# Attention states scaled in batches on VectorE, a later context transposition and six sums off GpSimd in a one-layer mixer and FFN kernel

## The chip, the cores and the metric

The kernel runs on one core of one Trainium2 chip. The metric is device time in microseconds, the median of three runs. "The profile" is the record of one further execution of the same program. TensorE is PE in it, its weight loads PEld, VectorE is DVE, ScalarE is ACT, GpSimd is POOL and SyncE is SP.

## The reference, cut to what matters

One layer: a mixer of three head groups (gated linear attention in both directions, a 2-D Fourier mix, a bidirectional linear recurrence) that share one input and one output projection, then a SwiGLU FFN. The 256 context tokens are used only for the states with which the scans of the 1024 latent tokens begin.

```python
def gla_scan(q, k, v, log_a, s0):            # forward; backward on flipped inputs
    ...
    b = jnp.cumsum(gc, axis=3)
    q_t = qc * jnp.exp(b)
    k_t = kc * jnp.exp(-b)
    k_end = kc * jnp.exp(b_last - b)
    attn = jnp.where(mask, jnp.einsum('nbhik,nbhjk->nbhij', q_t, k_t), 0.0)
    o_intra = jnp.einsum('nbhij,nbhjv->nbhiv', attn, vc)

    def step(s, inp):
        q_n, k_n, v_n, d_n = inp
        o_n = jnp.einsum('bhik,bhkv->bhiv', q_n, s)
        s_new = s * d_n[:, :, 0, :, None] + jnp.einsum('bhjk,bhjv->bhkv', k_n, v_n)
        return s_new, o_n
    ...
def gla_final_state(k, v, log_a):            # the context's state
    b = jnp.cumsum(log_a, axis=1)
    w = jnp.exp(b[:, -1:] - b)
    return jnp.einsum('bthk,bthv->bhkv', k * w, v)

def combine_groups(o_gla, z_og, g_gla, z_f, h_rg, z_rg):
    y_gla = gla_norm_gate(o_gla, z_og, g_gla)
    y_f = fourier_mix(z_f)
    y_rg = h_rg * jax.nn.gelu(z_rg.astype(jnp.float32))
    return jnp.concatenate([y_gla, y_f, y_rg], axis=-1).astype(z_og.dtype)

# latent_mixer: s_f, s_b, hf0, hb0 come from the context
    o_f, _ = gla_scan(q, k, v, la_f, s_f)
    o_b_rev, _ = gla_scan(rev(q), rev(k), rev(v), rev(la_b), s_b)
    h_f, h_b_rev = rglru_bidir(u, w_rg_a, b_rg_a, w_rg_x, b_rg_x, rg_lam, hf0, hb0)
    return combine_groups(o_f + rev(o_b_rev), z_og, g_gla, z_f, h_f + rev(h_b_rev), z_rg)
```

## The kernel before

All products are fp32 split into a high and a low part, so each is three matmuls (`mm3`, lines L84, L85 and L86). The input projection is made in tiles: `z` tiles (weights stationary or moving, 512 columns) and `zn` tiles (256 columns, tokens on the partitions). `z_v1` makes the second half of v in `zn` tiles, `vN` and `vNc` hold v of the latent tokens and of the context.

**The context's states.** For each of two head pairs p and two directions d, `ctx_exp` makes the weighted keys `b_c` (scan L438, exponential, product L443, on DVE and ACT), `ctx_tr` transposes them on PE (L449) and copies them to `kw_c` on DVE (L451), and `ctx_state` multiplies them with v (L459) and copies the state `s_ctx` (L462).

**The latent states.** `gla_states(p)` runs per head pair. `gla_kT` transposes the weighted keys `Kt` (L509). `gla_kv` takes a direction and a half q of the sequence, which has four steps in q=0 and three in q=1: products `kv` on PE (L527), then a chain `tt` on DVE (L532), each step from the one before. Each `tt` is also scaled by `gs` into the state tile `St` that the attention reads (L518, two instructions of 64x128 on ACT for two heads). The state of the context, scaled, is the first entry: with it 8 entries in each of 4 (p, d), 64 instructions on ACT.

**The attention blocks.** `gla_block(p, n)` makes one of 8 blocks of 128 tokens: the decayed queries `qx` (L571; direction 0 on DVE from `qT`, direction 1 on POOL from `qTs`, a copy of `qT` with its halves of partitions exchanged by DMA), `attn` (L575, PE), mask `am` (L577, L578, DVE), then `o` (L582 reads `St` and `qx`, L583 reads `am` and v). Direction 1 runs from the end, so block 0 needs the last entry of its chain. Between the blocks `fill` puts `z` tiles on PE: the queries of the second head pair, then the Fourier input.

**The recurrence.** `rg_ctx` and `rg_gates` make gates (`gate_ps`, L600, PE) with ACT functions behind, `rg_scan` scans on DVE (L644) and adds the two directions on POOL (L648, 128x1024, twice). `ada_row` sums eight slices of a weight (L658, DVE, `ada_acc`) and brings them to PE as `row_ps` (L669).

**The Fourier part.** `fourier` folds its input on DVE and POOL (`ze`, `zo`, `zfold`, L816 to L824), multiplies on PE (`Z_ps` L837, `y_ps` L850). `z_rg` makes `yfr` by a gelu on ACT from the next `zn` tiles, multiplied with the recurrence on DVE (L807). The output projection `o_ps` and the FFN (`prod`, `dn`) follow.

The program is written in the order of the functions; a scheduler with a model of the engines then sets each engine's order, within what pools allow: PSUM has 4 tiles of the kind `mm` and 4 of the kind `aux`. An engine works its own queue strictly in that order. So an instruction that waits holds up all that stands behind it on its engine. Line numbers are those of the kernel before; in the kernel after they are one to two higher from L518 on.

Of the kernel before, what the change touches and what calls it, by code (L numbers as in the profile page):

```python
# [16 lines left out]
P = 128  # L17
# [21 lines left out]
def tile_trunk(ctx: ExitStack, tc: tile.TileContext, A: dict):  # L39
    nc = tc.nc  # L40
    V, S, G, PE = nc.vector, nc.scalar, nc.gpsimd, nc.tensor
# [12 lines left out]
    def hp(shape=(P, 512), dt=F32, name="hp"):  # L54
        t = pool.tile(list(shape), dt, tag="hp", bufs=NHP, name=name)
        names["hp"].add(t.name)
        return t

    def sm(name, n=1):
        bufs = {3: 4, 4: 8, 8: 14}.get(n, 24)  # L60
        return pool.tile([P, n], F32, tag=f"sm{n}", bufs=bufs, name=name)

    def mm(name="mm"):
        return psum.tile([P, 512], F32, tag="mm", bufs=4, name=name)

    def aux(name="aux"):
        return psum.tile([P, 512], F32, tag="aux", bufs=4, name=name)
# [27 lines left out]
    def fl(ap, d):  # L95
        return ap[:, ::-1] if d else ap
# [129 lines left out]
    R = [slice(h * 64, (h + 1) * 64) for h in range(2)]  # L226
# [132 lines left out]
    def z_v1(blocks, c=False):  # L359
        z_N(w_v[1], 256, lambda ps, m: S.copy(vNc[1] if c else vN[1][m // 4][:, m % 4:m % 4 + 2, :], ps), blocks, c)  # L360
# [68 lines left out]
    s_ctx = [[None] * 2 for _ in range(2)]  # L429
# [35 lines left out]
    Ex, Kt, St = [[None] * 2 for _ in range(2)], [[None] * 2 for _ in range(2)], [[None] * 2 for _ in range(2)]  # L465

    def kt_begin(p):
        Kt[p] = [pg(name="Kt") for _ in range(2)]
        exchange(Kt[p][1], kT[p])
# [31 lines left out]
    def order(q):  # L501
        return range(4 * q, min(4 * q + 4, 7))
# [9 lines left out]
        return kn, last  # L512

    def gla_kv(p, d, q, kn, gs, tprev):
        def state(m, t):
            n = (7 - m) if d else m
            for h in range(2):
                S.mul(St[p][h ^ d][R[h], n, :], t[R[h]], gs[R[h], m:m + 1])  # L518

        if q == 0:  # L520
            state(0, s_ctx[p][d])
            tprev = s_ctx[p][d]
        kv = aux("kv")
        for i, m in enumerate(order(q)):
            n = (7 - m) if d else m
            for h in range(2):
                PE.matmul(kv[R[h], i * P:(i + 1) * P], kn[:, i * P + h * 64:i * P + (h + 1) * 64],  # L527
                          vN[p][n // 4][:, n % 4, (h ^ d) * P:((h ^ d) + 1) * P], start=True, stop=True)
        t4 = hp((P, 4, P), name="tt")
        for i, m in enumerate(order(q)):  # L530
            tt = t4[:, i, :]
            V.scalar_tensor_tensor(tt, tprev, gs[:, m:m + 1], kv[:, i * P:(i + 1) * P], op0=ALU.mult, op1=ALU.add)  # L532
            state(m + 1, tt)
            tprev = tt
        return tprev

    def gla_states(p):
# [14 lines left out]
    qT, qTs = [], []  # L552
# [13 lines left out]
    def gla_block(p, n):  # L566
        cs = slice(n * P, (n + 1) * P)
        qx, am = hp((P, 2, P), name="qx"), hp((P, 2, P), name="am")
        for d in range(2):
            for h in range(2):  # L570
                (G if d else V).tensor_mul(qx[R[h], h ^ d, :], (qTs if d else qT)[p][R[h], cs], Ex[p][d][R[h], cs])  # L571
        at = [aux("attn")[:, 0:256].rearrange("p (d i) -> p d i", d=2) for _ in range(2)]
        for d in range(2):
            for h in range(2):
                mark = PE.matmul(at[h][:, d, :], Kt[p][d][R[h], cs], qx[R[h], h ^ d, :], start=True, stop=True)  # L575
        for h in range(2):
            V.tensor_mul(am[:, h, :], at[h][:, 0, :], wmask)  # L577
            V.copy_predicated(am[:, h, :], imask, at[1 - h][:, 1, :])  # L578
        o = mm("o")
        for h in range(2):  # L580
            oc = o[:, h * P:(h + 1) * P]
            PE.matmul(oc, qx[:, h, :], St[p][h][:, n, :], start=True, stop=False)  # L582
            PE.matmul(oc, am[:, h, :], vN[p][n // 4][:, n % 4, h * P:(h + 1) * P], start=False, stop=True)  # L583
        ss = sm("oss", 2)
        jk = pool.tile([P, P], mybir.dt.bfloat16, tag="jk", bufs=1, name="jk")
        for h in range(2):
            S.activation(jk, o[:, h * P:(h + 1) * P], AF.Square, accum_out=ss[:, h:h + 1])
        r = rstd(ss, P, "ors", 2)
        if n % 4 == 0:
            on[p][n // 4] = pg((P, 4, 256), name="on")  # L590
        for h in range(2):
            V.tensor_scalar_mul(on[p][n // 4][:, n % 4, h * P:(h + 1) * P], o[:, h * P:(h + 1) * P], r[:, h:h + 1])
        return mark
# [21 lines left out]
    hR = []  # L615
# [25 lines left out]
    def rg_scan(blk, d, part):  # L641
        a, tr, ti = part
        rg_input(a, tr, ti)
        V.tensor_tensor_scan(fl(a, d), fl(a, d), fl(ti, d), h0[:, 2 * d + blk:][:, 0:1], op0=ALU.mult, op1=ALU.add)  # L644
        if d == 0:
            hR.append(a)
        else:
            G.tensor_add(hR[blk], hR[blk], a)  # L648


    def ada_row(c0, fn):
# [65 lines left out]
        vN[1][i] = pg((P, 4, 256), name="vN")  # L717
    w_q = [w_T(C_Q)]
    bs = [ctx_exp(p, d) for p, d in PD]
    z_v1(range(4))  # L720
    kws = [ctx_tr(b) for b in bs]
    for (p, d), kw in zip(PD, kws):
        ctx_state(p, d, kw)
    z_v1(range(4, 8))
    kt_begin(0)
    w_q.append(w_T(C_Q + P))
    def z_steps(w, h, ev):
# [47 lines left out]
    zf = [pg(name="zf") for _ in range(2)]  # L775
# [33 lines left out]
    def fourier(zf, blk):  # L809


        e, o = pg(name="ze")[:, 0:513], hp(name="zo")
        V.tensor_copy(e[:, 0:513:512], zf[:, 0:513:512])
        G.memset(o[:, 0:1], 0.0)
        rv = zf[:, 513:1024][:, ::-1]
        V.tensor_add(e[:, 1:512], zf[:, 1:512], rv)  # L816
        G.tensor_sub(o[:, 1:512], zf[:, 1:512], rv)
        f = pg((P, 4, 256), name="zfold")
        er, orv = e[:, 257:513][:, ::-1], o[:, 257:512][:, ::-1]
        V.tensor_add(f[:, 0, :], e[:, 0:256], er)  # L820
        V.tensor_sub(f[:, 1, :], e[:, 0:256], er)
        G.memset(f[:, 2:4, 0:1], 0.0)
        G.tensor_sub(f[:, 2, 1:], o[:, 1:256], orv)
        G.tensor_add(f[:, 3, 1:], o[:, 1:256], orv)  # L824
        cols = sm("fcol", 3)
        jk = hp(name="fjk")[:, 0:256]
        V.tensor_mul(jk, f[:, 0, :], alt)
        V.tensor_reduce(cols[:, 0:1], jk, axis=mybir.AxisListType.X, op=ALU.add)
        V.tensor_add(cols[:, 0:1], cols[:, 0:1], e[:, 256:257])
        V.tensor_copy(cols[:, 1:2], e[:, 256:257])  # L830
        V.tensor_copy(cols[:, 2:3], o[:, 256:257])
        Z = pg((P, 4, 2, P), name="Zcs")
        for s in range(2):
            ps = aux("Z_ps")
            for q in range(2):
                for i in range(2):
                    PE.matmul(ps[:, (2 * q + i) * P:(2 * q + i + 1) * P], f[:, 2 * s + q, i * P:(i + 1) * P], (Cd, Sd)[s],  # L837
                              start=True, stop=True)
            S.copy(Z[:, 2 * s:2 * s + 2].rearrange("p q i n -> p (q i n)"), ps)
        pc = aux("fc_ps")  # L840
        PE.matmul(pc[:, 0:2], Cd, cols[:, 0:2], start=True, stop=True)
        PE.matmul(pc[:, 2:3], Sd, cols[:, 2:3], start=True, stop=True)
        cc = sm("fcc", 3)
        V.tensor_copy(cc, pc[:, 0:3])
        yy = []
        for s in range(2):
            ps = aux("y_ps")
            for q in range(2):
                for i in range(2):
                    PE.matmul(ps[:, q * 256:(q + 1) * 256], Z[:, 2 * s + q, i, :], dft[s][:, q, i, :], start=i == 0, stop=i == 1)  # L850
            yy.append(ps.rearrange("p (q m) -> p q m", q=2))
        c, s = yy
        t = hp((P, 2, 256), name="yc")
        V.scalar_tensor_tensor(t[:, 0, :], alt, cc[:, 1:2], c[:, 0, :], op0=ALU.mult, op1=ALU.add)
        V.scalar_tensor_tensor(t[:, 1, :], alt, cc[:, 2:3], s[:, 1, :], op0=ALU.mult, op1=ALU.add)
        parts = (t[:, 0, :], s[:, 0, :]), (c[:, 1, :], t[:, 1, :])
        for q, (yc, ys) in enumerate(parts):
            for j in range(2):
                m = slice(j * P, (j + 1) * P)
                V.tensor_sub(yfr[j][:, blk, q::2], yc[:, m], ys[:, m])  # L860
            m = slice(1 - q, 129 - q)
            V.tensor_add(yfr[3][:, blk, q::2][:, ::-1], yc[:, m], ys[:, m])
            m = slice(129 - q, 256)
            V.tensor_add(yfr[2][:, blk, 2 - q::2][:, ::-1], yc[:, m], ys[:, m])
        V.tensor_copy(yfr[2][:, blk, 0:1], cc[:, 0:1])
# [450 lines left out]
    w = t_split(0)  # L1316
# [6 lines left out]
    for f in range(NFF):  # L1323
# [13 lines left out]
        w = wn  # L1337
# [92 lines left out]
```

## Time and profile before

| | |
|---|---|
| median of 3 runs | 1158.56 us (1156.19 to 1158.96) |
| the profiled execution, its own time | 1158.2 us |
| its span, first to last instruction | 1156.1 us |
| PE busy | 1090.0 us, 94% |
| DVE busy | 808.6 us, 70% |
| ACT busy | 504.6 us, 44% |
| POOL busy | 107.1 us, 9% |
| mean granted clock of TensorE | 0.968 |

The profiled execution is 2.1 us longer than its span; the stretch of the program that the change touches lies between 150 and 350 us of it, and the output projection begins at 381 us. Shares of busy time are means over stages with different limits. What is read is therefore where PE stands idle inside that stretch, what ended the idle time, and at which clock PE went on: 1.00 is the upper of two levels (2.4 GHz), 0.50 the lower (1.2 GHz), and a mean between them tells how much of a window was spent at each.

### The profile page before, as it was taken

The numbers are of one execution on the slowest core, as the hardware profiler recorded it, in microseconds if no ns is written. First come the engines' busy times: TensorE is split into PE (matmuls) and PEld (weight loads), VectorE is DVE, ScalarE is ACT, GpSimd is POOL, SyncE is SP. The second block draws the span as 40 slices with busy tenths as digits, with TensorE's granted clock in tenths as the row PEclk, the third lists the DMA queues.
The fourth block names the chain that finished last, engine by engine and source line by source line (L and its number), as shares of the span: only waits on it lengthen the run. The fifth ranks groups of instructions, "written<-read, shape, count | busy, mean of one in ns | idle before, by whom it ended". The sixth has DMA issues, their size and how long they took to land.

```text
span 1156.1 us, 15092 instructions
## 1 busy us (share of the span) xinstructions
PE 1090.0 (94%) x5514; PEld 904.8 (78%) x5514; DVE 808.6 (70%) x1383; ACT 504.6 (44%) x962; POOL 107.1 (9%) x133
## 2 busy tenths in 40 slices
PE   4899999989999999959999999999999999999877
PEld 2798886867789888748878888888888888888755
DVE  3474693648878366897788778776777658782795
ACT  3451867486364356653323233333323244470251
POOL 2210001214220001550000000000000000000100
PEclk8899998989999999969999999999999999999989
DMA  9803211213526223342382324232423479581681
GB/s 329 293 20 113 71 47 45 50 26 106 167 76 240 71 94 109 110 127 60 97 283 98 107 85 134 85 119 74 137 86 100 159 263 328 175 272 74 231 278 73
DMA packets 119970, 156.42 MB, mean 135 GB/s; under 512 B 8276, under 2 KB 70996, under 8 KB 119896
## 3 DMA queue, kind: packets, MB, share of 16 engines
q1 hardware_dynamic: 106536, 128.72, 34.4%
q10 hardware_dynamic: 13360, 26.75, 6.8%
q8 instruction: 43, 0.70, 0.2%
q14 instruction: 31, 0.25, 0.1%
HBM read 124.50 MB, written 28.57 MB: 132 GB/s over the span
## 4 chain that ended last, share of the span: by engine, by line
PE 79%; DVE 10%; ACT 4%; DMA 4%; issue 2%; POOL 0%; SPq 0%; DVEq 0%; POOLq 0%; ACTq 0%
PE prod L84 11%; PE prod L86 11%; PE prod L85 11%; PE dn L85 5%; PE dn L84 5%; PE dn L86 5%; PE z L84 3%; PE o_ps L86 3%; PE o_ps L84 3%; PE o_ps L85 2%; PE z L85 2%; PE z L86 2%; DMA wraw<-in_w_in 2%; ACT St L518 2%; PE zn L84 2%
## 5 line engine op out<-in xcount | busy, mean ns | idle before, releaser
L85 PE MATMUL dn<-dr,dl 128*128 128x512 f32 x308 | 122.8, 399 | 7.0 <-DVE dr L1178 6.9
L86 PE MATMUL dn<-dr,dl 128*128 128x512 f32 x308 | 121.8, 396 | 0.0
L84 PE MATMUL dn<-dr,dl 128*128 128x512 f32 x308 | 114.3, 394 | 3.1 <-ACT dr L1177 3.1
L116 POOL TENSOR_TENSOR rs<-rst,mhalf 128x1 f32<-128x1 f32 x34 | 21.6, 636 | 730.4 <-DVE rst L114 730.4
L85 PEld LDWEIGHTS dn<-dr,dl 128*128 128x128 f32 x308 | 58.7, 191 | 23.5 <-DVE dr L1178 11.6
L85 PE MATMUL zn<-w_lo,hl 128*128 128x256 f32 (+1 forms) x256 | 74.6, 293 | 0.0
L84 PE MATMUL zn<-w_hi,hl 128*128 128x256 f32 (+1 forms) x256 | 74.0, 291 | 0.2 <-ACT yfr L77 0.2
L86 PE MATMUL zn<-w_hi,hl 128*128 128x256 f32 (+1 forms) x256 | 73.7, 291 | 0.0
L84 PE MATMUL prod<-a,b_hi 128*128 128x512 f32 x176 | 69.8, 396 | 1.4 <-ACT b_hi L91 1.4
L84 PEld LDWEIGHTS dn<-dr,dl 128*128 128x128 f32 x308 | 58.5, 190 | 15.9 <-ACT dr L1177 3.5
L85 PE MATMUL prod<-a,b_hi 128*128 128x512 f32 x176 | 69.2, 393 | 0.0
L84 PE MATMUL prod<-s,wb_hi 128*128 128x512 f32 x176 | 68.9, 391 | 0.0
L85 PE MATMUL prod<-s,wb_hi 128*128 128x512 f32 x176 | 68.5, 389 | 0.0
L86 PE MATMUL prod<-s,wb_lo 128*128 128x512 f32 x176 | 68.3, 389 | 0.0
L86 PEld LDWEIGHTS dn<-dr,dl 128*128 128x128 f32 x308 | 59.0, 192 | 11.8
L86 PE MATMUL prod<-a,b_lo 128*128 128x512 f32 x176 | 68.1, 392 | 0.0
L84 PE MATMUL z<-hl,w_hi 128*128 128x512 f32 x160 | 65.2, 407 | 0.0
L85 PE MATMUL z<-hl,w_hi 128*128 128x512 f32 x160 | 63.9, 400 | 0.0
L1110 ACT CAST b<-wf_raw 128x512 fp32r<-128x512 f32 x22 | 13.7, 622 | 115.0 <-PE prod L86 105.4
L86 PE MATMUL z<-hl,w_lo 128*128 128x512 f32 x160 | 63.6, 398 | 0.0
L1178 DVE TENSOR_TENSOR dl<-h,dl 128x512 fp32r<-128x512 f32 x77 | 52.6, 683 | 14.9 <-ACT dl L1177 14.8
L1177 ACT CAST dl<-h 128x512 fp32r<-128x512 f32 x77 | 47.6, 619 | 18.3 <-issue 6.4
(351 smaller groups left out, 2856.0 us busy)
## 6 DMA issues: line engine op xcount, KB each, us to landing
ada_raw<-in_w_ada SPq DMA_DIRECT2D x48, 512.0 KB, 6.2
h<-hd SPq DMA_DIRECT2D x77, 256.0 KB, 4.8
wd_raw<-in_w_down SPq DMA_DIRECT2D x77, 256.0 KB, 5.1
hd<-c ACTq DMA_DIRECT2D x55, 256.0 KB, 2.1
wf_raw<-in_w_gate SPq DMA_DIRECT2D x25, 512.0 KB, 4.0
wf_raw<-in_w_up SPq DMA_DIRECT2D x22, 512.0 KB, 4.7
wraw<-in_w_in SPq DMA_DIRECT2D x16, 512.0 KB, 4.8
xb<-in_x SPq DMA_DIRECT2D x8, 512.0 KB, 8.0
```

What stands on the lines that cost most here:

```text
L84: PE.matmul(out, lh, rh, start=start, stop=False)
L85: PE.matmul(out, lh, rl, start=False, stop=False)
L86: return PE.matmul(out, ll, rh, start=False, stop=stop)
L116: G.tensor_tensor(out=r, in0=t, in1=mhalf.to_broadcast([P, cols]), op=ALU.pow)
L518: S.mul(St[p][h ^ d][R[h], n, :], t[R[h]], gs[R[h], m:m + 1])
L1110: S.copy(hi, u[:, 4:8])
L1177: S.copy(t[:, 0, :], raw)
L1178: V.tensor_sub(t[:, 1, :], raw, t[:, 0, :].bitcast(F32))
```

## The change

1. `gla_kv`: the 64 scalings on ACT become 24 products on DVE, with `gs` broadcast over 128 columns: for each (p, d) two of 64x128 for the context's entry, two of 64x512 behind the four steps of q=0, two of 64x384 behind the three steps of q=1. In direction 1 the written entries run backward.
2. All eight `zn` tiles of `z_v1` are issued ahead of `ctx_tr` and `ctx_state`, where it was four ahead and four behind.
3. The 32 `qx` of direction 1, the two adds of the recurrence and six sums of the Fourier fold go from POOL to DVE.

```diff
@@ gla_kv
-        def state(m, t):
-            n = (7 - m) if d else m
+        def states(m, w, t):
+            n = slice(8 - m - w, 8 - m) if d else slice(m, m + w)
             for h in range(2):
-                S.mul(St[p][h ^ d][R[h], n, :], t[R[h]], gs[R[h], m:m + 1])
+                V.tensor_mul(fl(St[p][h ^ d][R[h], n, :], d), t[R[h]], gs[R[h], m:m + w].unsqueeze(2).to_broadcast([64, w, P]))
         if q == 0:
-            state(0, s_ctx[p][d])
             tprev = s_ctx[p][d]
+            states(0, 1, tprev.unsqueeze(1))
...
             V.scalar_tensor_tensor(tt, tprev, gs[:, m:m + 1], kv[:, i * P:(i + 1) * P], op0=ALU.mult, op1=ALU.add)
-            state(m + 1, tt)
             tprev = tt
+        w = len(order(q))
+        states(4 * q + 1, w, t4[:, 0:w, :])
         return tprev
@@ gla_block
-                (G if d else V).tensor_mul(qx[R[h], h ^ d, :], (qTs if d else qT)[p][R[h], cs], Ex[p][d][R[h], cs])
+                V.tensor_mul(qx[R[h], h ^ d, :], (qTs if d else qT)[p][R[h], cs], Ex[p][d][R[h], cs])
@@ rg_scan
-            G.tensor_add(hR[blk], hR[blk], a)
+            V.tensor_add(hR[blk], hR[blk], a)
@@ the program's order
-    z_v1(range(4))
+    z_v1(range(8))
     kws = [ctx_tr(b) for b in bs]
     for (p, d), kw in zip(PD, kws):
         ctx_state(p, d, kw)
-    z_v1(range(4, 8))
@@ fourier
-        G.tensor_sub(o[:, 1:512], zf[:, 1:512], rv)
+        V.tensor_sub(o[:, 1:512], zf[:, 1:512], rv)
...
-        G.tensor_sub(f[:, 2, 1:], o[:, 1:256], orv)
-        G.tensor_add(f[:, 3, 1:], o[:, 1:256], orv)
+        V.tensor_sub(f[:, 2, 1:], o[:, 1:256], orv)
+        V.tensor_add(f[:, 3, 1:], o[:, 1:256], orv)
```

Three places in the engines' order matter below. First PE at the context's transposes, of the kernel before (`cm` holds the identity):

```order
L449 MATMUL ctx_tr<-cm,b_c 128x128 x2
L84 MATMUL zn<-w_hi,hl_492 128x256
L459 MATMUL ctx_st<-vNc,kw_c 64x128 x4
L85 MATMUL zn<-w_lo,hl_492 128x256
L86 MATMUL zn<-w_hi,hl_500 128x256
L84 MATMUL zn<-w_hi,hl_493 128x256
L85 MATMUL zn<-w_lo,hl_493 128x256
L86 MATMUL zn<-w_hi,hl_501 128x256
L459 MATMUL ctx_st<-vNc,kw_c 64x128 x8
```

and the same place after:

```order
L84 MATMUL zn<-w_hi,hl_494 128x256
L85 MATMUL zn<-w_lo,hl_494 128x256
L86 MATMUL zn<-w_hi,hl_502 128x256
L449 MATMUL ctx_tr<-cm,b_c 128x128 x8
L84 MATMUL z<-hl_487,w_hi 128x512
L85 MATMUL z<-hl_495,w_hi 128x512
L86 MATMUL z<-hl_487,w_lo 128x512
```

Before, the four pairs of transposes stood among `zn` matmuls, the first pair with 61 of them still behind it; after, all eight stand together behind the last `zn`, and the sixteen `ctx_st` follow 21 `z` matmuls later.

Second DVE at the state chain of the second head pair, before (tt_2432 and tt_2476 are direction 0, the other two direction 1):

```order
L532 SCALAR_TENSOR_TENSOR tt_2456<-tt_2456,gs_2381,kv_2447 128x128
L532 SCALAR_TENSOR_TENSOR tt_2476<-tt_2476,gs_2367,kv_2469 128x128
L532 SCALAR_TENSOR_TENSOR tt_2493<-tt_2456,gs_2381,kv_2486 128x128
L571 TENSOR_TENSOR qx_2540<-qT_1989,la_711 64x128 x2
L532 SCALAR_TENSOR_TENSOR tt_2493<-tt_2493,gs_2381,kv_2486 128x128 x2
L577 TENSOR_TENSOR am_2541<-attn_2546,cm_65 128x128
```

and after (tt_2412 and tt_2444 are direction 0, tt_2430 and tt_2457 direction 1):

```order
L533 SCALAR_TENSOR_TENSOR tt_2457<-tt_2430,gs_2361,kv_2450 128x128
L573 TENSOR_TENSOR qx_2500<-qT_1969,la_711 64x128
L519 TENSOR_TENSOR St_2373<-tt_2444,gs_2347 64x384
L519 TENSOR_TENSOR St_2374<-tt_2444,gs_2347 64x384
L573 TENSOR_TENSOR qx_2500<-qT_1969,la_711 64x128
L573 TENSOR_TENSOR qx_2500<-qTs_1970,la_712 64x128 x2
L533 SCALAR_TENSOR_TENSOR tt_2457<-tt_2457,gs_2361,kv_2450 128x128 x2
L579 TENSOR_TENSOR am_2501<-attn_2506,cm_65 128x128
L573 TENSOR_TENSOR qx_2539<-qT_1969,la_711 64x128
L519 TENSOR_TENSOR St_2374<-tt_2457,gs_2361 64x3x128
L519 TENSOR_TENSOR St_2373<-tt_2457,gs_2361 64x3x128
```

The batches of `St` and the `qx` of direction 1 now stand inside the chain, and the last two batches stand behind the first mask of block 8, which waits for PE. On PE, `o` of block 8 stood directly behind `gate_ps` before; now `attn` of blocks 8 and 9 stand ahead of it.

Third PE at the Fourier part, before:

```order
L84 MATMUL zn<-w_hi,hl_490 128x256
L85 MATMUL zn<-w_lo,hl_490 128x256
L86 MATMUL zn<-w_hi,hl_498 128x256
L837 MATMUL Z_ps<-cm,zfold 128x128 x8
L84 MATMUL zn<-w_hi,hl_491 128x256
L85 MATMUL zn<-w_lo,hl_491 128x256
L86 MATMUL zn<-w_hi,hl_499 128x256
```

and after:

```order
L84 MATMUL zn<-w_hi,hl_491 128x256
L85 MATMUL zn<-w_lo,hl_491 128x256
L86 MATMUL zn<-w_hi,hl_499 128x256
L84 MATMUL zn<-w_hi,hl_492 128x256
L85 MATMUL zn<-w_lo,hl_492 128x256
L86 MATMUL zn<-w_hi,hl_500 128x256
L837 MATMUL Z_ps<-cm,zfold 128x128 x8
```

The matmuls of `hl_491` open a new `zn` tile. Before, `Z_ps` stood ahead of that tile's first matmul; now the tile's first nine matmuls stand ahead of `Z_ps`.

## Rows read from the trace of the kernel before

**Rows 1.** The page's head: span; busy time and its share of each engine.

```profile
span 1156.1 us, 15092 instructions
PE 1090.0 (94%) x5514; PEld 904.8 (78%) x5514; DVE 808.6 (70%) x1383; ACT 504.6 (44%) x962; POOL 107.1 (9%) x133
```

**Rows 2.** Waits of PE, 130 to 382 us: waited for; us, times, longest.

```profile
PE o L582 <- ACT St L518: 4.4, 1, 4.4
PE ctx_tr L449 <- DVE b_c L443: 2.6, 1, 2.6
PE gate_ps L600 <- ACT qT L559: 2.0, 1, 2.0
PE Z_ps L837 <- DVE zfold L820: 2.0, 2, 1.7
PE row_ps L669 <- DVE ada_acc L658: 0.8, 1, 0.8
```

**Rows 3.** Windows: us; busy (count) of PE, PEld, DVE, ACT, POOL; clock, DMA, GB/s.

```profile
160.00:170.00 10.00, 9.40 (x75) 8.49 (x76) 9.89 (x37) 4.74 (x8) 0.00 (x0) 0.83 0.22 55
190.00:200.00 10.00, 8.04 (x37) 5.05 (x35) 4.60 (x16) 9.12 (x21) 1.22 (x3) 0.77 0.33 79
200.00:210.00 10.00, 10.00 (x42) 8.07 (x42) 5.71 (x15) 7.08 (x14) 0.70 (x1) 0.72 0.01 2
250.00:260.00 10.00, 5.66 (x18) 4.21 (x19) 2.60 (x7) 9.79 (x18) 0.00 (x0) 0.67 0.00 0
```

**Rows 4.** Timeline (start, us, instruction) of PE, then DVE, at the context.

```profile
157.58 0.28 PE L84 MATMUL zn<-w_hi,hl 128*128 128x256 f32 x1
157.70 0.28 PE L85 MATMUL zn<-w_lo,hl 128*128 128x256 f32 x1
...
163.72 0.42 DVE L443 TENSOR_TENSOR b_c<-b_c,kTcs 128x256 f32<-128x256 f32 x1
```

**Rows 5.** Timeline of ACT, then POOL, around the two head pairs' states.

```profile
192.96 0.60 ACT L559 ACTIVATE qT<-z 128x512 f32<-128x512 f32 x1
...
242.67 11.53 ACT L518 ACTIVATE St<-tt,gs 64x128 f32<-64x128 f32 x28 [2.76 <-DVE tt L532]
...
186.67 3.65 POOL L571 TENSOR_TENSOR qx<-qTs,la 64x128 f32<-64x128 f32 x7 [0.80 <-DMA qTs<-qT]
```

**Rows 6.** Groups of DVE, 140 to 385 us: busy us, mean ns; idle before.

```profile
L571 DVE TENSOR_TENSOR qx<-qT,la 64x128 f32<-64x128 f32 x32 | 10.0, 313 | 0.4
...
L486 DVE TENSOR_TENSOR la<-la,bA 128x512 f32<-128x512 f32 x4 | 2.7, 681 | 0.0
...
L497 DVE TENSOR_TENSOR Kt<-Kt,kT 128x1024 f32<-128x1024 f32 x2 | 2.4, 1216 | 0.0
```

**Rows 7.** Windows of the two head pairs' stretches and of the fullest DVE.

```profile
180.30:202.40 22.10, 20.14 (x120) 14.55 (x118) 10.13 (x34) 19.71 (x45) 4.55 (x10) 0.84 0.21 49
242.30:309.70 67.40, 62.15 (x323) 46.63 (x319) 50.28 (x111) 38.70 (x87) 20.00 (x25) 0.95 0.33 112
...
280.00:290.00 10.00, 10.00 (x56) 7.49 (x56) 9.86 (x25) 3.57 (x14) 5.23 (x8) 1.00 0.49 164
```

**Rows 8.** Timeline: DVE and PE, second head pair; the output projection's start.

```profile
246.25 0.73 DVE L532 SCALAR_TENSOR_TENSOR tt<-tt,gs,kv 128x128 f32<-128x128 f32 x2
...
246.32 3.60 PE L600 MATMUL gate_ps<-uT,gates 128*128 128x512 f32 x8
...
381.30 0.40 PE L84 MATMUL o_ps<-wo_hi,yh 128*128 128x512 f32 x1
```

**Rows 9.** Timeline of PE and DVE at the Fourier part.

```profile
330.31 2.02 PE L837 MATMUL Z_ps<-cm,zfold 128*128 128x128 f32 x16 [0.29 <-DVE zfold L820]
332.57 0.39 PE L84 MATMUL zn<-w_hi,hl 128*128 128x256 f32 x1 [0.23 <-ACT yfr L77]
...
339.29 3.30 DVE L807 TENSOR_TENSOR yfr<-yfr,a 128x256 f32<-128x256 f32 x3 [2.24 <-POOL a L648]
...
342.59 0.41 DVE L807 TENSOR_TENSOR yfr<-yfr,a 128x256 f32<-128x256 f32 x1
```

## The prediction

> **What bounds the kernel now.** I read the page's head first: PE is busy for 94% of the span, DVE for 70%, ACT for 44%, POOL for 9% [rows 1]. So the kernel can only become shorter where PE stands idle or runs at its lower clock. The next view is PE's waits in the stretch of the change: 4.4 us for the last `St` on ACT, 2.6 for `b_c` on DVE, 2.0 for the copy of `qT` on ACT, 2.0 for `zfold`, 0.8 for `ada_acc` [rows 2]. With the 0.2 us for `yfr` [rows 9] these make 12.0 us. The third view is the clock by windows: it stands below 1.00 behind each of the three longest single waits, and there alone in this stretch [rows 3]. A mean of 0.83 over 10 us is 3.4 us at half speed, which costs 1.7 us of work. So the three places cost: 1.7 us behind the 2.6 us wait; 2.3 + 2.8 = 5.1 us behind the 2.0 us wait; at most 3.3 us behind the 4.4 us wait (at most, since part of that window is the wait itself). Behind the 1.7 us wait for `zfold` no row shows a lower clock. Waits and clock together make 22 us, and no gain can be larger unless something outside this stretch changes.
>
> **Prices.** The new DVE instructions are ordinary products with both inputs in SBUF. Measured on DVE: 64x128 takes 0.31 us, 128x512 0.68, 128x1024 1.22 [rows 6], 128x256 0.42 [rows 4]. A batch 64x512 has the columns of 128x512, so 0.68; 64x384 lies between 0.42 and 0.68, say 0.55. The `gs` factor is broadcast, as `bA` is in the 0.68 us row [rows 6], and direction 1 is written backward; for the second no row gives a price, and I take none. Added to DVE: 8 x 0.31 + 8 x 0.68 + 8 x 0.55 = 12.3 us of `St`; 32 x 0.31 = 10.0 us of `qx`; 2 x 1.22 = 2.4 us of the recurrence's adds; 2 x 0.68 + 4 x 0.42 = 3.0 us of Fourier sums. That is 27.7 us. Taken from ACT: 28 instructions in 11.53 us are 0.41 us each [rows 5], so 64 make 26 us. POOL's own time had no wait of PE on it in rows 2; what it loses is worth nothing by itself.
>
> **Place A, the context.** PE ended its `zn` matmuls at 157.98 and waited 2.6 us with 61 `zn` matmuls of that same half still behind the first transpose. Those come 0.12 us apart [rows 4], 7.3 us in all, so after the change PE reaches `ctx_tr` at 165.3. The last of the four `b_c` was ready at 164.14 [rows 4]. The wait goes, and with it the cause of the low clock: 2.6 + 1.7 = **4.3 us**. What is late next is the chain `kw_c`, `ctx_st`, `s_ctx`, which now starts some 5 us later on PE and whose DVE copies stand behind two products of 128x1024, `w_lo` and `Kt` (1.22 us each [rows 6]). 39 `z` matmuls and the `kv` of the chain come behind it, and the states of the context are needed by the first `tt` alone. I price this at nothing; without that cover it costs at most the two copies ahead of it, 2.4 us. No DMA moves with `z_v1`.
>
> **Place B, first head pair, to the first `o`.** The 2.0 us wait is ACT's: `qT` was copied at 192.96 [rows 5] because `St` scalings stand ahead of it on ACT, and the gates' functions behind it, so `gate_ps` could not be emptied. The scalings leave ACT, which was busy for 19.7 of 22.1 us here [rows 7]; 28 x 0.41 = 11.5 us go. At most 2.0 + 5.1 = 7.1 us are to be had. DVE was busy for 10.1 of these 22.1 us and gets 4 x 0.68 + 4 x 0.55 + 8 x 0.31 = 7.4 us. It fits, but not without friction: chain, batches, `qx` and masks stand in one queue, and block 0 needs the last batch of direction 1. The eight gates with two blocks of attention are also a sparse stretch for PE, in which short waits of some tenths will stay. I take **5.0 us**, between 2.0 (the clock falls as before) and 7.1. One wait is added to DVE: the first `qx` of direction 1 waits for the exchange DMA, which POOL did for 0.8 us [rows 5]; behind it on DVE stand two `tt`, the first masks and the last batch. The copy of `qT` is earlier now, so I price it at 0, at most 0.8.
>
> **Place C, second head pair, 242 to 310.** The `tt` chain ended at 246.98 on DVE [rows 8], but ACT scaled until 254.2 [rows 5], while PE's gates were done at 249.92 [rows 8]. PE side: 4.4 + 3.3 + 0.8 = 8.5 us at most. DVE side: busy for 50.3 of 67.4 us [rows 7], and it gets 6.1 of `St`, 16 x 0.31 = 5.0 of `qx`, 1.2 of the recurrence and 0.7 of the Fourier sums, 13.0 us. That makes 63.3 of 67.4. If DVE had to work without a pause, this stretch could become 4.1 us shorter. In DVE's order the last batches stand behind the mask of block 8, so `o` of block 8 comes no earlier than about 11 us after the first `tt`, as now; the gain is that two blocks of `attn` stand ahead of it on PE. I take **4.2 us**, range 0 to 8.5.
>
> **Place D, Fourier, 310 to 381.** Waits of 0.3, 0.2 and 1.7 us stood here. But the `zn` tile that waits for `yfr` hid behind 2.0 us of `Z_ps` [rows 9]. With `Z_ps` behind its ninth matmul, that tile waits for the gelu itself: from 330.02 to 332.57 less the 0.0 to 0.3 us by which it can come earlier, about 2.3 to 2.5 us. The waits cancel to within half a us: 2.3 to 2.5 new, and 0.3 + 0.2 + 1.7 = 2.2 gone, the 1.7 because POOL's add held up DVE's queue for 2.24 us ahead of `yfr` [rows 9]. What comes with a wait of 2.5 us is the low clock, 1.7 us by place A. Net 2.2 - 2.4 - 1.7 = **-1.9 us**.
>
> **A rule weighed.** Three `yfr` products took 3.30 us, 1.1 us each, while POOL worked on the Fourier sums; the next, of the same size, took 0.41 us [rows 9]. The Trainium skill (SBUF — State Buffer, "SBUF: two separate sides") says of this that a DVE operation with two SBUF inputs and a GpSimd operation share a port pair as an exclusive lock, so that one blocks the other for its whole length. The trace agrees, 1.1 against 0.41 us. By that rule the move from POOL gives DVE back 3.30 - 3 x 0.41 = 2.1 us here, and the forecast would be 1144.9 if all of it lay on the path; without it, it stays as the sum below has it.
>
> **The sum.** 4.3 + 5.0 + 4.2 - 1.9 = 11.6 us, from the profiled execution's 1158.2 us: 1146.6. That execution is 0.4 us below the median of the runs, so the forecast is **1147.0 us**. Behind the output projection's start [rows 8] nothing of the order changes that costs anything; waits for DVE there start from PE's own products and shift with them.
>
> **Rivals.**
> *Clean.* DVE's queue is no obstacle and no new low clock comes: all of A and B, 5.5 of C's 8.5 us and nothing lost in D, 4.3 + 7.1 + 5.5 = 16.9 us, 1141.7. For it: DVE idles 12 of 22 us in place B. Against: several short waits in B.
> *The clock stays low.* The waits in B and before block 8 break into smaller ones, but PE still drops to half speed as in rows 3: 11.6 less 5.1 in B and 2.5 of the 3.3 in C, 4.0 us, 1154.6. For it: PE keeps its sparse order of gates and attention there. Against: no single wait there is as long as 2.0 us.
> *The wait moves.* DVE's chain replaces ACT's for the same time in B and C, and A's 4.3 us are lost to D's 2.5 + 1.7 us: 1158.6 - 4.3 + 4.2 = 1158.5. For it: `o` of block 8 comes no earlier after the first `tt`. Against: `attn` and `z` tiles stand ahead of it.
> *DVE becomes the bound,* the other side. Between 242 and 310 us DVE must carry 63.3 us, and in 280 to 290 it is already busy for 9.86 of 10 [rows 7]. If its 17.1 idle us are not usable because each is a wait for PE in a fixed order, the 13.0 us lie on the path; with A and B gaining 9.3 and D losing 1.9, the time is 1158.6 + 13.0 - 9.3 + 1.9 = 1164.2. It decides against the kernel once less than 5.6 of the 17.1 us can be used, since then A's and B's gain of 9.3 less D's 1.9 is spent. Against: `z` tiles are kept as filling between the blocks, and PE works for 62.15 of the 67.4 us [rows 7], so DVE's pauses are there because PE is the later one. The Trainium skill (Perfetto Trace Analysis, "Optimizing Scalar/DVE Operations") speaks for this rival: from a saturated DVE work may better go to ScalarE, the reverse of this change, and where DVE is not saturated but holds up other engines, smaller instructions may finish sooner, the reverse of batches. The trace agrees with its condition in single windows (9.86 of 10 us) and not over the span (70%).
>
> **How the numbers follow.** Forecast (1144 to 1150.5) 0.50; clean 0.18; low clock 0.18; wait moves 0.08; DVE as bound 0.06. The range reaches from the clean case, 1 us below it, to 1156, which holds the low-clock case and leaves out the two last. Faster by over 0.3% (3.5 us, about what a measurement of this kernel can tell from no change) is below 1155.1: the first two and most of the third, 0.82; within 0.3%: 0.12; slower: 0.06.
>
> **What would show it.** Right: no wait of PE for `b_c`, none for `qT` or for `St` on ACT, a granted clock near 1.00 from 160 to 260, and a new wait of some 2.5 us of `zn` for `yfr`. Wrong: PE waiting over 2 us for DVE's `St` or masks, a clock near 0.7 where the gates stand, DVE at 10 of 10 through 240 to 300 with PE idle, or `o_ps` starting later than 375 us; it starts at 381.3 [rows 8], by the sum at 369.7.

## The result and the profile after

The changed kernel takes 1151.41 us, the median of 6 runs (1148.07 to 1152.98), against 1157.44 us for 6 runs of the kernel before. The ratio of the two kernels is 0.9936 with an interval of 0.9921 to 0.9951, so the change saves about 7.4 us; the two medians alone lie 6.0 us apart. The forecast was 1147.0 us, 11.6 us saved, with a range of 1140.7 to 1156.0. The profiled execution of the kernel after is the slowest of its six, 1152.98 us with a span of 1151.2.

The page's head of the kernel after (span; busy us of each engine and its share), which answers to [rows 1]:

```profile
span 1151.2 us, 15035 instructions
PE 1089.0 (95%) x5514; PEld 904.0 (79%) x5514; DVE 826.8 (72%) x1447; ACT 479.4 (42%) x898; POOL 76.9 (7%) x93
```

PE's waits from 120 to 382 us, kernel after (waited for; us, times, longest), which answer to [rows 2]:

```profile
PE zn L84 <- ACT yfr L77: 2.5, 1, 2.5
PE attn L577 <- DVE qx L573: 1.8, 5, 0.7
PE o L585 <- DVE am L580: 1.6, 3, 0.7
PE row_ps L671 <- DVE ada_acc L660: 0.5, 1, 0.5
PE k_tr L509 <- PE k_tr L509: 0.4, 1, 0.4
PE z L84 <- ACT qT L754: 0.4, 1, 0.4
```

The waits for `b_c`, for `qT` and for `St` are gone, 9.0 us in all, and the wait of 2.5 us for `yfr` is there. New are eight short waits for DVE's `qx` and `am`, 3.4 us together.

To see where time was gained, the same matmul is looked up in both traces, with the same set of matmuls ahead of it, and its start is compared. The five points in the kernel before are: a `zn` matmul at 100.01 us, ahead of everything the change touches; a `z` matmul at 187.51, between places A and B; a `z` matmul at 233.71, between B and C; the first `row_ps` at 309.69, between C and D; and `o_ps` at 381.30. Each column is the kernel's time for that stretch less that of the kernel before, in one profiled execution; negative is a gain. "Rest" is everything behind `o_ps`. Only in e3 does the order differ at a point: six `kv` products stand ahead of the second one in place of six `z` matmuls, so e3's A and B are rough and their sum, -1.7, is not. The stretch ahead of A, which no edit touches, differs by -0.4 to +1.5 us between executions.

| kernel | ratio to before | ahead of A | A | B | C | D | rest | `o_ps` at |
|---|---|---|---|---|---|---|---|---|
| forecast | 0.990 | 0 | -4.3 | -5.0 | -4.2 | +1.9 | 0 | 369.7 |
| after | 0.9936 | +1.0 | -5.0 | -1.8 | -1.2 | +1.5 | +0.6 | 375.8 |
| e1 | 0.9868 | -0.4 | -5.0 | -3.4 | -3.5 | +1.5 | -3.5 | 370.5 |
| e2 | 0.9894 | +1.5 | -5.0 | -3.7 | -2.2 | -0.6 | -1.6 | 371.4 |
| e3 | 0.9977 | +0.7 | -4.7 | +3.0 | -0.1 | -0.1 | +0.1 | 380.1 |
| e4 | 0.9900 | +0.5 | +0.4 | -5.9 | -5.3 | 0.0 | -1.1 | 371.1 |
| e5 | 0.9852 | +0.4 | -5.0 | -3.4 | -5.0 | 0.0 | -3.2 | 368.3 |
| e6 | 0.9882 | +0.4 | -5.0 | -3.4 | -5.2 | -0.6 | 0.0 | 367.5 |
| e7 | 1.0031 | -0.3 | 0.0 | +2.0 | +5.1 | 0.0 | +0.5 | 388.1 |
| e8 | 0.9882 | +1.0 | -5.0 | -2.0 | -5.2 | -0.1 | -2.5 | 370.0 |
| e9 | 0.9978 | +1.0 | +0.5 | -3.5 | +3.5 | 0.0 | -3.5 | 382.8 |
| e10 | 0.9905 | +0.1 | -5.0 | -1.7 | -1.3 | +1.5 | -2.5 | 375.0 |
| e11 | 0.9857 | -0.1 | -5.0 | -3.4 | -5.0 | -0.6 | -3.3 | 367.2 |
| e12 | 0.9930 | +0.9 | +0.5 | -4.5 | -2.9 | +1.5 | -2.6 | 376.7 |

Place A gave about what was forecast, D cost about what was forecast, B and C fell short by 3.2 and 3.0 us. Windows of the kernel after tell the first thing about B and C (us; busy and count of PE, PEld, DVE, ACT, POOL; granted clock; DMA share; GB/s), which answers to [rows 3] and [rows 7]; the last row is the whole of place C:

```profile
190.00:200.00 10.00, 9.48 (x39) 7.29 (x39) 8.33 (x25) 8.84 (x19) 0.70 (x1) 0.83 0.01 4
...
250.00:260.00 10.00, 9.65 (x56) 7.43 (x56) 9.67 (x26) 4.41 (x12) 0.79 (x1) 1.00 0.08 26
270.00:280.00 10.00, 8.62 (x38) 6.14 (x39) 9.81 (x26) 2.89 (x10) 2.26 (x3) 0.83 0.64 203
...
227.96:302.69 74.73, 71.37 (x384) 53.77 (x382) 62.13 (x153) 32.34 (x74) 9.75 (x13) 0.98 0.33 107
```

A clock of 0.83 over 10 us is 3.4 us at the lower of the two levels, which costs 1.7 us of work. There is one such piece in B and one in C. In C, DVE works 62.1 of 74.7 us. It is not full, yet PE waits for it.

DVE and PE in the kernel after, at block 8 (timeline: start, us, instruction; in brackets the idle time ahead of it and what ended it). The first four rows are DVE's queue, one behind the other, the last is PE:

```profile
245.96 1.11 DVE L519 TENSOR_TENSOR St<-tt,gs 64x384 f32<-64x384 f32 x2
246.99 0.28 DVE L573 TENSOR_TENSOR qx<-qT,la 64x128 f32<-64x128 f32 x1
247.31 1.23 DVE L640 SCALAR_TENSOR_TENSOR ti<-ti,uT 128x1024 f32<-128x1024 f32 x1
248.45 0.28 DVE L573 TENSOR_TENSOR qx<-qTs,la 64x128 f32<-64x128 f32 x1
...
248.78 0.49 PE L577 MATMUL attn<-qx,Kt 64*128 64x128 f32 x2 [0.49 <-DVE qx L573]
```

The query that PE waits for is a 0.28 us instruction (the one at 248.45), and in DVE's queue it stands behind a product of the recurrence of 1.23 us, which is wanted later. The two batches ahead of that (1.1 us) are the last ones of direction 1; `o` of block 8 reads them and starts at 247.38, 0.3 us after they end.

### The profile page after: what moved, and what is told of

It is laid out like the page before. It is cut to its first block, busy times and chain, and to the rows that moved or that the text cites. A ratio compares the mean times of both kernels' runs of the same rounds, so it can differ in the third digit from the quotient of the medians.

```text
span 1151.2 us, 15035 instructions
## 1 busy us (share of the span) xinstructions
PE 1089.0 (95%) x5514; PEld 904.0 (79%) x5514; DVE 826.8 (72%) x1447; ACT 479.4 (42%) x898; POOL 76.9 (7%) x93
## 4 chain that ended last, share of the span: by engine, by line
PE 78%; DVE 11%; DMA 6%; ACT 2%; issue 2%; SPq 0%; DVEq 0%; POOL 0%; POOLq 0%; ACTq 0%
PE prod L84 11%; PE prod L85 11%; PE prod L86 11%; PE dn L85 5%; PE dn L86 5%; PE dn L84 5%; PE z L84 3%; PE zn L84 3%; PE zn L85 3%; PE zn L86 3%; PE z L85 3%; PE o_ps L84 3%; PE o_ps L86 3%; PE o_ps L85 3%; PE z L86 3%; DMA wraw<-in_w_in 2%
## 5 line engine op out<-in xcount | busy, mean ns | idle before, releaser
L86 PEld LDWEIGHTS dn<-dr,dl 128*128 128x128 f32 x308 | 59.0, 192 | 11.9
L1178 ACT CAST dl<-h 128x512 fp32r<-128x512 f32 x77 | 47.6, 619 | 18.2 <-DMA h<-hd 5.9
```

Source lines behind the costliest of these rows:

```text
L86: return PE.matmul(out, ll, rh, start=False, stop=stop)
L1178: S.copy(t[:, 0, :], raw)
```

## The experiments

Theory Q: the queries of direction 1 lose on DVE what the batches gain, since they stand in its queue between `am` and PE, while POOL made them beside it. Rivals: the Fourier sums on DVE are the loss (D); the later transposes gain nothing that lasts; and, formed after the first runs, a part of the difference lies in the FFN, far behind the change (F).

### Queries back on POOL: e1, e8, and alone e7

```diff
e1  -  V.tensor_mul(qx[...], ...)    +  (G if d else V).tensor_mul(qx[...], ...)
e8  -  V.tensor_mul(qx[...], ...)    +  (G if d and p else V).tensor_mul(qx[...], ...)
e7  (from the kernel before)
    -  (G if d else V).tensor_mul(qx[...], ...)    +  V.tensor_mul(qx[...], ...)
```

> The kernel after, with the 32 products qx of direction 1 back on POOL; everything else as after. Theory Q (the queries): of the gain that did not come in the attention stages, most is lost because qx, masks and state batches stand in one queue on DVE; then PE's waits for qx and for am (1.8 and 1.6 us after) shrink below 1 us together, the low clock near 276 us goes, and the ratio to before is 0.987 to 0.991. Theory S (the states): it is the 24 state batches on DVE that hold up the masks, the queries are harmless; then the waits stay within 1 us of those after and the ratio is 0.993 to 0.995.

Measured: 0.9868 (0.9853 to 0.9883), 8 us better than the kernel after and a little more than Q gave. PE's waits for `qx` and `am` fall only from 3.4 to 1.8 us; a low-clock piece in C did not go but stands at 270 us. Only 1.6 us of the gain are in B and 2.3 in C; 4.1 us are behind `o_ps`, which Q had not foreseen.

> The kernel after, with the queries of the second head pair alone back on POOL, those of the first on DVE. By the records of the run with all queries on POOL, 3 us of the 8 were lost in the first pair's stage and 5 in the second's (place C with the low clock behind it). So theory Q expects 4 to 6 us less than after, ratio 0.988 to 0.990; if the loss is made in the first pair and only shifts the rest, 0.992 to 0.994.

Measured: 0.9882 (0.9864 to 0.9901). C gains 5.2 us, as in the kernels with all queries on POOL (5.0 to 5.2 in e5, e6 and e11; e1 has its low-clock piece there), and B stays at 2.0: the price in C belongs to the second pair's 16 queries. The whole of place C of e8, to be held against the last window of the kernel after:

```profile
227.76:298.51 70.75, 68.52 (x383) 52.85 (x381) 59.32 (x138) 32.21 (x75) 21.41 (x29) 1.00 0.34 112
```

Four us shorter with nearly the same matmuls, DVE 2.8 us less busy, the clock at 1.00.

> The kernel before, with the queries of direction 1 moved from POOL to DVE and nothing else. Theory Q (a full queue on DVE is what makes the queries dear): with the states still on ACT, DVE has room, and the move costs 0 to 3 us, ratio 0.999 to 1.003. Rival (each query on DVE lengthens a block's chain by itself, whatever else stands there): 5 to 9 us slower, ratio 1.004 to 1.008.

Measured: 1.0031 (1.0016 to 1.0046), a loss of 3.6 us, just past the upper edge of Q and short of the rival. PE's waits for `am` rise to 2.0 us. The profiled execution, 1165.2 us, is 4.3 us above the median of 1160.9 and has low-clock pieces between 250 and 300 us, so its 7 us in B and C are more than the median shows: 5.1 of them are work lost to more low clock than in the kernel before. What is left is 0.3 us in B and 1.7 in C. In C that is not much less than the 2.4 us found below with the batches on DVE, so that a full queue is what makes the queries dear is not shown.

### One part alone: e3, e4, e5, e12

```diff
e3  before +  z_v1(range(8)) ahead of ctx_tr
e4  before +  gla_kv with states(), 24 products on DVE
e5  e3 and e4 together (all of part 3 left as before)
e12 after  with  z_v1(range(4)) ahead of ctx_tr, z_v1(range(4, 8)) behind ctx_state
```

> The kernel before, with all of z_v1 ahead of the context's transposes and nothing else changed. Theory A (as forecast): the wait of 2.6 us and the low clock behind it go and nothing is late, 4.3 to 5 us, ratio 0.9957 to 0.9965, still there at the output projection's start (376 to 377 us). Rival (given back): the states of the context come later, so that ACT's chain of scalings, which bounds the stage behind it, comes later too, and the ratio is 0.998 to 1.000.

Measured: 0.9977 (0.9968 to 0.9987), between the two expectations and near "given back". A gains 4.7 us and B gives back 3.0. Windows and a wait of e3:

```profile
190.00:200.00 10.00, 7.79 (x26) 4.55 (x25) 5.24 (x19) 9.75 (x23) 1.80 (x4) 0.52 0.12 27
200.00:210.00 10.00, 10.00 (x35) 7.96 (x36) 4.99 (x12) 6.43 (x13) 1.73 (x3) 0.62 0.01 2
```

```profile
PE o L582 <- ACT St L518: 4.4, 1, 4.4
PE gate_ps L600 <- ACT qT L559: 2.0, 1, 2.0
```

ACT's scalings still set both waits, and the clock behind the shorter one is 0.52 and 0.62, lower than the 0.77 and 0.72 of [rows 3]: 8.6 us of work lost in place of 5.1. These 3.5 us cover the 3.0 that B gave back, so in this execution it was the clock that took A's gain, and a later chain on ACT, the rival's reason, is not shown.

> The kernel before, with the states scaled in batches on DVE and nothing else changed (queries and sums stay on POOL, the transposes where they were). Theory Q: the waits for St on ACT (4.4 us) and for qT (2.0 us) and most of the low clock go without new waits for DVE over 1 us; 6 to 9 us, ratio 0.992 to 0.995. Theory S: the batches hold up the masks, PE waits over 2 us for am and qx, and the ratio is 0.997 or more.

> The kernel before with parts 1 and 2 of the change, and all queries and sums left on POOL. Theory A2 (the transposes pay once ACT's chain is gone): the 4.3 us of the context, given back in the run with the later transposes alone, are kept here, since the stage behind no longer waits for scalings on ACT; 11.6 us of the batched states plus 3.5 to 5, ratio 0.9855 to 0.987. Rival: given back again, because the chain of states itself starts later; ratio 0.9885 to 0.9905.

Measured: e4 0.9900 (0.9885 to 0.9916), more than expected; e5 0.9852 (0.9837 to 0.9868), 1140.87 us, slightly more than expected because of its FFN. Part 1 alone is worth 11.2 us in B and C together. In e5 the gains of A and B are not the sum of each alone: A 5.0 and B 3.4 against B 5.9 without A, with the clock at 1.00 in B both times. The whole of place C and PE's four longest waits (120 to 382 us) of e5:

```profile
225.73:296.71 70.98, 68.75 (x383) 52.86 (x382) 59.20 (x132) 33.02 (x76) 26.45 (x31) 1.00 0.34 114
```

```profile
PE Z_ps L838 <- DVE zfold L821: 2.0, 2, 1.7
PE row_ps L671 <- DVE ada_acc L660: 0.8, 1, 0.8
PE attn L577 <- POOL qx L573: 0.8, 1, 0.8
PE o L585 <- DVE am L580: 0.6, 1, 0.6
```

> The kernel after, with the context's transposes where they were before. By the start of the output projection the later transposes should be worth 3 to 5 us (373 to 376 us after would become 378 to 380 us). But the scheduler here puts wa_hi ahead of four of the six casts by itself, so theory F expects 4 to 5 us back in the FFN and a ratio near that of after, 0.992 to 0.995; without theory F it is 0.996 to 0.998.

Measured: 0.9930 (0.9916 to 0.9943), as expected with theory F and no different from the kernel after. But its FFN is 3.2 us better ("rest" -2.6 against +0.6). The kernel after with the FFN's order put right, e10 below, has 0.9905, so with a like order there the later transposes are worth about 2.9 us beside parts 1 and 3. `o_ps` starts at 376.7 us, earlier than the 378 to 380 expected: what A loses, B and C win back (4.5 and 2.9 us), because no low-clock piece fell there. So in place C e12 and e4, which differ by part 3 alone, can be compared at full clock. The whole of place C with PE's three longest waits in it, first e12, then e4:

```profile
230.56:303.61 73.05, 69.67 (x384) 52.84 (x382) 61.51 (x152) 33.07 (x74) 9.78 (x13) 1.00 0.33 111
...
PE o L585 <- DVE am L580: 1.6, 3, 0.6
PE attn L577 <- DVE qx L573: 1.3, 2, 0.7
PE row_ps L671 <- DVE ada_acc L660: 0.5, 1, 0.5
```

```profile
228.77:299.46 70.69, 68.45 (x383) 52.84 (x382) 59.32 (x134) 32.99 (x75) 27.04 (x31) 1.00 0.35 114
...
PE row_ps L671 <- DVE ada_acc L660: 0.8, 1, 0.8
PE attn L577 <- POOL qx L573: 0.8, 1, 0.8
PE o L585 <- DVE am L580: 0.6, 1, 0.6
```

73.05 - 70.69 = 2.4 us for part 3 on DVE and no clock in it. That it is the queries of the second pair shows e8: there everything else of part 3 is on DVE, and place C takes 70.75 us. DVE's busy time differs by 2.2 us, so its idle time is the same, 11.5 and 11.4 us, and PE's three waits add up to 3.4 us against 2.2. What DVE got more to do went into the time, though it was idle for 11 us.

### The Fourier sums back on POOL: e2, e6

```diff
e2  -  V.tensor_sub(o[...]); V.tensor_sub(f[:, 2, ...]); V.tensor_add(f[:, 3, ...])
    +  G.tensor_sub(o[...]); G.tensor_sub(f[:, 2, ...]); G.tensor_add(f[:, 3, ...])
e6  e1 and e2 together (of part 3 only the recurrence's adds remain on DVE)
```

> The kernel after, with the six sums of the Fourier fold back on POOL; the order of PE then has Z_ps ahead of the tile that waits for yfr, as before. Theory D (order): the 2.5 us wait of zn for yfr and the low clock behind it are made by that order; both go, the later wait for zfold (1.7 us before) may return in part, and the ratio is 0.990 to 0.993. Rival (port): what the order gives back, POOL's sums take again by holding up DVE's products with two inputs (1.1 instead of 0.41 us each), and the ratio is 0.9935 to 0.9955.

Measured: 0.9894 (0.9877 to 0.9912), more than D gave. D itself gains 2.1 us over the kernel after, the wait for `yfr` falls from 2.5 to 0.2 us. B is 1.9 us better with the same queries on DVE: its low-clock piece isn't there. Another 2.2 us are behind `o_ps`.

> The kernel after with the queries and the Fourier sums back on POOL; only the recurrence's two adds of part 3 stay on DVE. If the two costs are independent (queries 8 us in the attention stages, Fourier order 4 to 5 us behind them), the ratio is 0.982 to 0.9845; if POOL, with both again, holds up DVE in the attention and Fourier stages, it is 0.986 to 0.988, no better than the queries alone on POOL.

Measured: 0.9882 (0.9866 to 0.9899), next to the second by the number, but not by its reason. The mixer adds up as hoped: `o_ps` at 367.5 us, earlier than e5's 368.3, so the recurrence's adds are well placed on DVE: D gains 0.6 us in e2, e6 and e11, which have the adds on DVE and the sums on POOL, and 0.0 in e5. But "rest" is 0.0 where e5 has -3.2, and e5 is the faster kernel.

### The FFN's start: e9, e10, e11

120 us behind the output projection's start PE waits for ACT's cast `wa_hi`. PE's waits from 470 to 520 us, kernel before, then after, then e5:

```profile
PE prod L84 <- ACT wa_hi L91: 11.4, 1, 11.4
```

```profile
PE prod L84 <- ACT wa_hi L91: 11.0, 1, 11.0
```

```profile
PE prod L84 <- ACT wa_hi L91: 6.3, 1, 6.3
```

No line of this place was edited. In the order of ACT's queue, six casts of `s` stand ahead of `wa_hi` in the kernels before, after, e3, e4, e6 and e7 (wait 11.0 to 11.9 us), four in e2 and e8 (9.8 and 9.2), two in e1, e5 and e12 (6.3 to 6.9). The scheduler, which orders by its own model of time, moved them; the mixer ahead is all that differs between these kernels. The six casts in the kernel before (ACT's timeline, then two rows of DVE's):

```profile
506.23 0.71 ACT L924 CAST s<-s 128x256 fp32r<-128x256 f32 x2
507.69 0.71 ACT L924 CAST s<-s 128x256 fp32r<-128x256 f32 x2 [0.75 <-POOL s L1059]
509.39 0.71 ACT L924 CAST s<-s 128x256 fp32r<-128x256 f32 x2 [0.98 <-POOL s L1062]
512.97 1.04 ACT L91 CAST wa_hi<-wf_raw 128x1024 fp32r<-128x1024 f32 x1 [2.87 <-DVE wf_raw L1115]
...
511.06 1.27 DVE L925 TENSOR_TENSOR s<-s,s 128x256 fp32r<-128x256 f32 x2
512.26 0.68 DVE L1115 TENSOR_TENSOR wf_raw<-wf_raw 128x512 f32<-128x512 f32 x1
```

By its row, `wa_hi` waited last not for a cast but for DVE's `wf_raw`, which stands behind DVE's share of the same token sums. So the place of the sums on both engines goes with the wait, and the next runs move it.

Three kernels force two casts ahead of `wa_hi`, in the kernels before (e9), after (e10) and e6 (e11):

```diff
-  S.copy(hi, raw)
+  his.append(S.copy(hi, raw))
...
   w = t_split(0)
-  all_of(s_last)
+  with tc.issue_after(his[-2].ins):
+      all_of(s_last)
```

(with one more step of `s_last` issued ahead of `t_split`).

> The kernel before, with nothing of the change; only at the start of the FFN ACT's cast wa_hi is put ahead of the last four casts of the token sums (those of s4 and s3, which POOL makes). Theory F (an order far behind the change): the wait of PE for wa_hi was 11.0 to 11.9 us in the kernels with six such casts ahead of it, 9.3 and 9.8 with four, 6.3 and 6.8 with two; here it falls from 11.4 to 6.2 to 7 us, and the ratio is 0.995 to 0.9965, though attention, context and Fourier are as before. Rival: the wait was shorter in those kernels because of what the change does ahead of it, and the cast order is a sign of it alone; then the wait stays at 10 us or more, ratio 0.998 to 1.001.

> The kernel after, with the same cast order at the start of the FFN. Theory F: 4 to 5 us less than after, ratio 0.989 to 0.991, with the output projection starting at about 376 us as after. Rival: as after, 0.993 to 0.995.

> Batched states and later transposes, the recurrence's adds on DVE, queries and Fourier sums on POOL (whose output projection started earliest, at 367.5 us), and the cast order of the FFN forced. Theory F: 4 to 5 us less than without the forced order (0.9882), ratio 0.983 to 0.985, the fastest so far. Rival: 0.987 to 0.989.

Measured: the wait becomes 5.9, 6.0 and 5.7 us as meant. The times: e9 0.9978 (0.9967 to 0.9990), less than expected; e10 0.9905 (0.9888 to 0.9921), as expected; e11 0.9857 (0.9841 to 0.9872), 1140.62 us, just short of it. "Rest" gains 3.1 to 3.5 us over the same kernel without the forced order, for about 5 us of wait; the ratios say 2.5 to 3.6. Why not more, a wait of e9 shows, and the windows of the FFN's start, kernel after and then e10:

```profile
PE prod L86 <- DVE wa_lo L94: 0.8, 1, 0.8
```

```profile
497.57:512.00 14.43, 3.41 (x9) 2.75 (x10) 13.29 (x18) 5.24 (x10) 4.96 (x4) 0.65 0.34 88
```

```profile
496.64:511.00 14.36, 7.63 (x19) 5.57 (x19) 11.87 (x16) 6.44 (x13) 9.38 (x6) 0.64 0.35 90
```

DVE's `wa_lo` is next in line, and the low clock lasts as long (0.65 and 0.64): in the kernel after it covered a wait, in e10 it covers twice the work.

e5 and e11 are equal within their intervals and beat both kernels: 1140.9 and 1140.6 us.

## Why the prediction was right or wrong

**Place A was right.** 4.3 us forecast, 5.0 measured (4.7 to 5.0 in every kernel with part 2; the others show a loss of 0.0 to 0.5). From 160 to 170 us the clock is 1.00 in all kernels with part 2 and 0.83 in all without. The chain behind, priced at nothing, cost nothing there. But A's gain doesn't last by itself: e3 keeps 0.0023 of the time, and the comparison of the kernel after with e12 finds nothing, because e12 has the better order in the FFN and no low-clock piece in B and C; against e10, with a like FFN, it finds 2.9 us. The sum added A and B as if each were free of the other. By the runs A and B together give 8.4 us at best (e5), B alone 5.9 (e4): what PE gains at A it partly spends at B, since ACT and DVE there don't get earlier by as much. That last clause is argued, not tested.

**Place B was the wrong size.** 5.0 forecast, 1.8 measured. The mechanism held: no wait for `qT`. Two things were missing. With A in place B has only 3.4 to 3.7 us to give (e1, e2, e5, e6, e11). The other 1.6 to 1.9 us are the low-clock piece at 194 to 197 us, ahead of which no wait is longer than 0.23 us. The queries of the first pair do not cost it by their order: e2 has them on DVE, the same short waits of up to 0.23 us, a clock of 1.00, and takes 3.7. Only without part 2 do they cost time by themselves, 1.4 us at full clock (e12 4.5, e4 5.9). The piece is in the kernel after, e8 and e10, which have these queries on DVE, not in e2 and e12, which have them too, and in none of the five kernels with part 1 and these queries on POOL. So they make it likelier at most, and why the clock fell stays open.

**Place C was wrong in one step**: "I take 4.2 us" from PE's side, because 63.3 of 67.4 us fitted. 1.2 us came. The prices were right: 64x512 took 682 ns, 64x384 550 (0.68 and 0.55 were taken). DVE's groups in the kernel after, 140 to 385 us (busy us, mean ns; idle before), which answer to [rows 6]:

```profile
L573 DVE TENSOR_TENSOR qx<-qTs,la 64x128 f32<-64x128 f32 x32 | 9.2, 286 | 0.9
L519 DVE TENSOR_TENSOR St<-tt,gs 64x512 f32<-64x512 f32 x8 | 5.5, 682 | 0.1
L519 DVE TENSOR_TENSOR St<-tt,gs 64x384 f32<-64x384 f32 x8 | 4.4, 550 | 0.1
L808 DVE TENSOR_TENSOR yfr<-yfr,a 128x256 f32<-128x256 f32 x8 | 3.0, 421 | 2.6 <-ACT yfr L77 2.5
```

What failed is reading a fit of busy time as a fit of order: idle time of DVE was counted as free for work that PE waits for. The 16 queries cost 4.0 us in C (e8), of which 2.4 come without the clock (e12 against e4, both at 1.00) and the rest is the low-clock piece at 276 to 279 us. The rival "DVE becomes the bound" had the right mechanism, idle time that a fixed queue can't use, at a fraction of its price: not the 13.0 us of all additions, but 2.4 for queries that were to take 5.0. The batches themselves cost nothing that shows (e4 gains 11.2 us with them), so this rival fell as it was worded. The Trainium skill (Perfetto Trace Analysis, "Optimizing Scalar/DVE Operations") says that work may go from a saturated DVE to ScalarE or even GpSimd. Here moving the queries to GpSimd paid (e1, e8) though DVE was not saturated, at 62.1 of 74.7 us. Its other rule, smaller instructions where an unsaturated DVE holds up other engines, no run tests: e4 changes the engine and the size of the scalings at once.

**Place D was right.** -1.9 forecast, -1.5 measured, by the step named: the wait of 2.5 us for `yfr` and a low clock behind it. The wait is set by where `Z_ps` stands on PE, and that by the engine of the Fourier sums: with them on POOL it is 0.2 us (e2, e6, e11). The low clock is behind it in the kernel after, e1, e10 and e12. In e8 the same wait has none behind it, and D costs nothing.

**The lock on the ports.** POOL's leaving gives DVE time: `yfr` fell from 694 to 421 ns as a mean of eight, 2.2 us in all where 2.1 were worked out (in e2, where POOL's next sums start only behind them, it is 422), and DVE's busy time rose by 18.2 us, not the 27.7 of the sum. The Trainium skill (SBUF — State Buffer, "SBUF: two separate sides") states this exclusive use, and the trace agrees. No gain in time is seen from it: the kernels with the queries or the Fourier sums back on POOL (e1, e2) are faster.

**"Behind the output projection's start nothing of the order changes that costs anything"** was right for the kernel after (+0.6 us, wait 11.4 to 11.0) and wrong as a rule: the edits of the mixer alone moved between +0.6 and -3.5 us there.

**The rivals.** Clean (1141.7 us) is the time of e5 and e11, but not in the mixer: `o_ps` starts there at 368.3 and 367.2 us, by the clean sum at 364.4, and 3.2 and 3.3 us come from the FFN. "The clock stays low" (1154.6) and "the wait moves" were each right in part: two pieces of low clock came back without any long wait, and 3.4 us of short waits on DVE took the place of ACT's. In the sum, 11.6 - 7.4 = 4.2 us are missing by the ratio, 5.1 up to `o_ps` in the profiled executions: 3.2 in B and 3.0 in C, less 0.7 more in A and 0.4 less lost in D. One sign of being wrong came true, `o_ps` later than 375 us (375.8). That the time still lies within the range is no sign that B and C were understood: the range was wide enough to hold both misses.

## What to carry to other kernels

Before small instructions go to an engine that is 84% busy (59.3 of 70.7 us, e4), look at what stands ahead of each in its queue and at who waits for it, not at its idle share: here 16 products of 0.3 us, each wanted at once by PE, cost 2.4 us at full clock, while the batches, fewer and larger, cost nothing that shows. Test the parts of a bundled change one by one: here the first gained 11.6 us alone (e4), the second 2.7 alone (e3) and beside the two others nothing (e12) or 2.9 (e10 against e12, with a like FFN), and the third lost 9.7 (the kernel after against e5), 3.8 of it in the FFN. With a scheduler that orders by its own model, compare the order far behind the edit too, since 2.5 to 3.6 us of a gain can come from there.

## What the runs showed of the hardware

The low clock doesn't follow from the wait ahead of it alone. The kernel before lost 5.1 us of work behind its wait of 2.0 us for `qT` [rows 2, 3]. In e9 the mixer is the same, with the same order on every engine up to `o_ps`, and PE's wait is there as well (timeline of e9):

```profile
195.14 1.20 PE L602 MATMUL gate_ps<-cx,gates 128*128 128x256 f32 x4 [1.94 <-ACT qT L561]
```

But the clock of e9 stays at 1.00 (windows):

```profile
190.00:200.00 10.00, 8.03 (x46) 5.43 (x44) 4.03 (x16) 9.08 (x21) 2.68 (x6) 1.00 0.33 79
200.00:210.00 10.00, 10.00 (x67) 8.46 (x65) 7.53 (x19) 9.05 (x23) 0.70 (x1) 1.00 0.01 2
```

So of the 7.1 us that the prediction saw in place B, 5.1 don't have to come with that wait; e3 and e7 lose more (8.5 and 6.8). Instead e9 lost 3.5 us more than the kernel before in C, to a low clock at 252 to 266 us, where the kernel before has it from 253 to 260. The other way round, the kernel after fell to the lower level at 194 us with no wait over 0.23 us ahead of it, and at 276 us behind waits of 0.7 and 0.6 us, while e5, e6 and e8 have waits as long in place C (0.8 and 0.6) at a clock of 1.00. The six executions of the kernel after spread over 4.9 us, and the mean clock goes with it roughly: 0.977 in the shortest, 0.973 in the longest, the profiled one. What decides between two such executions stays open. A price for "the clock behind a wait", read from one execution, should have this spread as its uncertainty.
